# Three value products moved into the preparation of the scan's blocks, fixed places for the scan's matrices, and two gate products in other places

## The chip, the cores and the metric

The kernel runs on one core of a Trainium2 chip, as one program in one launch. The metric is the time of one execution in device microseconds; three executions of the kernel before took 1086.29, 1088.93 and 1091.3 us, the median is 1088.93.

## The reference

One encoder layer is applied to two sequences with the same weights, of 1024 and 256 tokens, 1024 wide, in float32. The kernel treats them as 1280 tokens in 10 blocks of 128 and 20 chunks of 64. After an RMS norm one product with `w_in` gives the inputs of three groups of heads, whose outputs are joined, multiplied with `w_out`, and followed by a small embedding branch and a last norm:

```python
qkv = silu(centred_dwconv(a_qkv, conv_w))          # 5 taps; six heads, 3 x 384 channels
aq, ak, av = split(qkv); aq, ak = l2_normalize(aq), l2_normalize(ak)
o_a = rms_norm(gated_delta_rule(forward) + gated_delta_rule(backward)) * silu(a_gate)
o_b = head_layer_norm(retention(forward) + retention(backward)) * silu(b_gate)
o_c = window_attention(c_q, c_k, c_v, sink) * silu(c_gate)
h = h + concat(o_a, o_b, o_c) @ w_out
h = rms_norm(h + (p @ w_ple) * sigmoid(h @ w_pg))
```

The gated delta rule works chunk by chunk: for each chunk, head and direction a 64 x 64 triangular matrix is inverted, and a scan over the chunks carries a 64 x 64 state. Each scan step needs the inverse, the keys, the values, and three matrices that don't depend on the state: the decayed queries, the masked query-key product, and the decayed keys.

## The kernel before

**Dense products.** Every product with `w_in` is made tile by tile of 128 columns. `load_w` (L134) loads a weight tile by one DMA into the single buffer `raw` and splits it into `hi` and `lo`; `dense` (L171) makes 24 matmuls for each of three stretches of tokens (512, 512, 256): 8 slices of the inner dimension, and for each hi x xh, hi x xl and lo x xh. Then `evac` empties the PSUM bank. One such product is 72 matmuls on TensorE (PE); a stretch of tokens of it is called a block of dense work here.

**Stages.** First the nine tiles of `a_qkv` are made one after the other (L509 to L566, order 3, 4, 5, 0, 1, 2, 6, 7, 8: keys, queries, values). Each has a tail: four taps on VectorE (L525), a sigmoid in three ScalarE passes (L98), a product, and then for keys and queries the normalisation (L530 to L550), for values (L552 to L566) ten transposes, copies into the tile `vt`, and three stores to `VTD`. The tiles work in `ot`, rows 0 to 2 and 3 to 5 in turn.

Then `prep_stream` (L569) prepares the scan, from block 9 down to block 0 and for each of the two directions: gram products into PSUM, their transposes, decay factors `ge` on ScalarE, and from these the tile `at` (what is inverted) and the tile `l2`, which the trace calls `l` (the three matrices of the scan). `at` leaves by five DMAs, `l2` by one (L621), all on SP's queue. Behind blocks 5 and 0 comes `invert` (L399): a chain of some sixty VectorE operations for five blocks and both directions together, in `ot` rows 0 and 1, and a store of the inverse to `YDD`. `ge` shares two buffers with `vt`, and `l2` shares two with a tile of the normalisation.

Beside this run dense products as filler. A table says which, and `spread` (L440) draws from both streams in proportion to their lengths:

```python
PP = ["cq0", "cq1", 6, 7, 3, "ck", "cv", 4, 0, 5]                        # beside prep_stream
PB = [1, 2, "q0"]                                                        # beside attention
RS = [["k0", "v0"], ["q1"], ["k1", "v1"], ["k2"], ["v2"], ["q2"], []]    # beside retention
```

A number is a gate: 0 to 2 of the delta rule, 3 to 5 of retention, 6 and 7 of attention. A gate's `evac` (L464) copies the bank to `sz` (L468), makes the sigmoid in `sg`, multiplies, and for gates 0 to 5 stores `sg` to `GD` (L472); `sz` and `sg` have one buffer each. `cq0`, `cq1`, `ck`, `cv` are attention's, `q`, `k`, `v` are retention's.

Last, two streams are woven: `scan_stream` (L749) joins the halves of the inverses (`join`, L650) and makes 20 steps in both directions (`step`, L693); `fill` (L1089) makes attention with PB, then retention with RS. When both are done, `w_out`, `w_pg` and `w_ple` follow (L1126 on).

**What sets the order.** The engines' instructions are put in order when the program is built, by a scheduler that follows the order of the code, its priorities and a timeline of its own; each engine then works strictly in that order, and so does SP's queue of DMAs. A table entry that moves thus moves rows of every engine.

**The scan's matrices.** In `l2`, of shape (128, 2 chunks, 3 pairs of heads, 3 matrices, 64), the two heads of a pair lie on partitions 0 to 63 (`T`) and 64 to 127 (`B`). A step multiplies a whole 128-partition matrix that holds, for one head, the decayed queries in one half and the query-key product in the other. So matrix 0 holds queries in T and the product in B, matrix 1 the other way round, and each needs its own VectorE call per half (L611, L612, L615).

Of the kernel before, what the change touches and what calls it, by code (L numbers as in the profile page):

```python
# [8 lines left out]
F32 = mybir.dt.float32  # L9
# [8 lines left out]
NB = 10  # L18
NC = 20
# [17 lines left out]
PP = ["cq0", "cq1", 6, 7, 3, "ck", "cv", 4, 0, 5]  # L37
PB = [1, 2, "q0"]
RS = [["k0", "v0"], ["q1"], ["k1", "v1"], ["k2"], ["v2"], ["q2"], []]
# [14 lines left out]
def encoder_kernel(ctx: ExitStack, tc: tile.TileContext, I, O, dbg=None, upto=99):  # L54
# [405 lines left out]
    kreg = {}  # L460

    def product(n):
        if n in GCOL:
# [11 lines left out]
            return [(GCOL[n], 128)], evg  # L475
        if n[0] == "c":
# [19 lines left out]
    with tc.tile_pool(name="pa", reuse_waits="tile", bufs=2) as pa:  # L496
# [12 lines left out]
        order = [3, 4, 5, 0, 1, 2, 6, 7, 8]  # L509
        for i, ti in enumerate(order):  # L510
            z = i % 2
            if i == 2:
                beta_alpha(pa)
# [7 lines left out]

            dense(ahead.pop() if ahead else load_w([(ti * 128, 128)]), evac)
            G.memset(Y[:, 1024:1028], 0.0)
            for j in (0, 1, 3, 4):
                V.scalar_tensor_tensor(out=Y[:, 0:1284], in0=R[:, j:j + 1284], scalar=cw(ti, j),  # L525
                                       in1=Y[:, 0:1284], op0=MUL, op1=ADD)
            sigmoid(Z[:, 0:1284], Y[:, 0:1284])
            tt(V, Z[:, 0:1284], Z[:, 0:1284], Y[:, 0:1284], MUL)
            if ti < 6:
                p, isq = ti % 3, ti < 3  # L530
                S.activation(out=Y[:, 0:1284], in_=Z[:, 0:1284], func=AF.Square)
                for t0, n_t, o in SEGS:
                    for s0 in range(0, n_t, 512):
                        n = min(512, n_t - s0)
                        pn = ps("tr")
                        sq = pa.tile([128, 2, 512], F32R, tag="l2", name=nm("sq"))
                        ys = Y[:, o + s0:o + s0 + n]
                        S.copy(sq[:, 0, :n], ys)
                        tt(V, sq[:, 1, :n], ys, sq[:, 0, :n].bitcast(F32), SUB)
                        mm(pn[:, :n], onesR, sq[:, 0, :n], stop=False)  # L540
                        mm(pn[:, :n], onesR, sq[:, 1, :n], start=False)

                        rr = pa.tile([128, 512], F32, tag="ge", name=nm("rr"))
                        S.activation(out=rr[:, :n], in_=pn[:, :n], func=AF.Ln,
                                     scale=64.0 if isq else 1.0, bias=eps64 if isq else eps)
                        S.activation(out=rr[:, :n], in_=rr[:, :n], func=AF.Exp, scale=-0.5)
                        tt(V, kq[:, p, 1 if isq else 0, t0 + s0:t0 + s0 + n], Z[:, o + s0:o + s0 + n], rr[:, :n], MUL)
                if not isq:
                    nc.sync.dma_start(out=KND[:, :, p, :].rearrange("c p t -> p c t"),
                                      in_=kq[:, p, 0, :].rearrange("p (c t) -> p c t", c=NC))  # L550
            else:
                p = ti - 6  # L552
                for b0 in range(0, NB, 4):
                    nb = min(4, NB - b0)
                    o = b0 * 128 if b0 < 8 else 1028
                    pt = ps("tr")
                    for k in range(nb):
                        nc.tensor.transpose(pt[:, k * 128:(k + 1) * 128], Z[:, o + k * 128:o + (k + 1) * 128], ident)
                    pt4 = pt[:, 0:nb * 128].rearrange("p (b h e) -> p b h e", b=nb, h=2)
                    vt = pa.tile([128, 4, 2, 64], F32, tag="ge", name=nm("vt"))  # L560
                    for r in range(2):
                        rr = slice(64 * r, 64 * r + 64)
                        S.copy(vt[T, 0:nb, r], pt4[rr, :, 1])
                        V.tensor_copy(vt[B, 0:nb, r], pt4[rr, :, 0])
                    nc.sync.dma_start(out=VTD[b0 // 4][:, :, p, :].rearrange("c p e -> p c e"),
                                      in_=vt[:, 0:nb].rearrange("p b r e -> p (b r) e"))  # L566
        if dbg:
            dbg("kq", kq)
        def prep_stream():  # L569
            for b in reversed(range(NB)):  # L570
# [18 lines left out]
                for d in range(2):  # L589
# [661 lines left out]
```

## Time and profile before

| | us |
|---|---|
| Median of 3 executions | 1088.93 |
| The profiled execution | 1093.26 |
| Its span, from first to last instruction | 1091.5 |
| PE busy with matmuls | 1016.7 (93%) |
| VectorE (DVE) busy | 653.5 (60%) |
| ScalarE (ACT) busy | 511.8 (47%) |
| GpSimd (POOL) busy | 239.9 (22%) |
| Mean granted clock of PE | 0.96 of full speed |

The profile is one execution, taken by the hardware profiler. Its page gives busy times per engine, a row of 40 slices, and groups of instructions by line of the code; queries of the trace give the same for a stretch of time, list who waited for whom (an engine's idle time is put down to what ended it), and follow the chain of waits back from the last instruction. Line numbers are those of the kernel; L86 and L89 are helpers that make all matmuls and all two-operand VectorE calls, so there the names of the tiles tell the place (`mm` is the PSUM bank of a dense product, `tr`, `sa`, `sb` those of the smaller ones). SP is the queue from which nearly all DMAs are issued. A busy PE is not PE at its peak: the small matmuls of the scan take longer than their columns need, and the granted clock falls in places.

### The profile page before, as it was taken

How to read it: one execution, taken by the hardware profiler on the slowest of the kernel's cores; microseconds unless marked ns; L12 is line 12 of the kernel's file. 1: busy time of each engine (PE TensorE's matmuls, PEld its weight loads, DVE VectorE, ACT ScalarE, POOL GpSimd, SP SyncE). 2: the span in 40 equal slices, each digit the busy share in tenths (PEclk: the TensorE clock that was granted, in tenths of full speed). 3: DMA queues.
4: the chain of work that ended last, by engine and by line, in shares of the span. 5: the costliest groups of instructions: out<-in, count | busy, mean ns of one | idle time of the engine just before them, and what ended most of it. 6: DMA issues, size and time to landing. Idle time of an engine off the chain costs nothing.

```text
span 1091.5 us, 20976 instructions
## 1 busy us (share of the span) xinstructions
PE 1016.7 (93%) x7859; PEld 811.7 (74%) x7859; DVE 653.5 (60%) x1363; ACT 511.8 (47%) x1194; POOL 239.9 (22%) x406
## 2 busy tenths in 40 slices
PE   4999999999896879989999799999889999999996
PEld 3768878888775757767776677777657888888885
DVE  6766676477899769844756674565884333411333
ACT  7476776577456445334434522323341121444544
POOL 2001000022213011221232525644541000112311
PEclk9999999999999888989999799969889999999998
DMA  7112112367776354453553434563571430300211
GB/s 255 40 44 68 44 39 59 74 172 209 183 184 185 79 134 112 111 107 86 142 151 100 123 88 134 141 165 102 172 237 50 164 107 1 97 1 10 97 77 77
DMA packets 192991, 120.56 MB, mean 110 GB/s; under 512 B 104947, under 2 KB 171803, under 8 KB 192891
## 3 DMA queue, kind: packets, MB, share of 16 engines
q1 hardware_dynamic: 187994, 118.97, 39.9%
q8 instruction: 62, 1.02, 0.4%
q0 software_dynamic: 4896, 0.27, 0.4%
q14 instruction: 39, 0.31, 0.1%
HBM read 76.26 MB, written 42.91 MB: 109 GB/s over the span
## 4 chain that ended last, share of the span: by engine, by line
PE 66%; DVE 13%; DMA 10%; SPq 3%; ACT 3%; issue 3%; POOL 1%; DVEq 0%; ACTq 0%; POOLq 0%
PE mm L86 37%; PE sa L86 15%; PE sb L86 7%; PE tr L86 4%; DVE ot L89 3%; DMA ad<-at 2%; DVE l L89 2%; DMA yd<-ot 1%; DMA gd<-sg 1%; DVE ot L966 1%; SPq L618 1%; DMA yn<-yd 1%; PE tr L848 1%; DMA oo<-od 1%; DMA xt<-in_x_prompt 1%
## 5 line engine op out<-in xcount | busy, mean ns | idle before, releaser
L86 PE MATMUL mm<-xh,whi 128*128 128x512 f32 x720 | 268.1, 372 | 16.4 <-ACT sz L468 13.8
L86 PE MATMUL mm<-xl,whi 128*128 128x512 f32 x720 | 263.8, 366 | 0.0
L86 PE MATMUL mm<-xh,wlo 128*128 128x512 f32 x720 | 263.3, 366 | 0.0
L86 PEld LDWEIGHTS mm<-xh,whi 128*128 128x128 f32 x720 | 138.5, 192 | 42.7 <-ACT sz L468 16.4
L86 PEld LDWEIGHTS mm<-xh,wlo 128*128 128x128 f32 x720 | 138.2, 192 | 21.6 <-issue 0.5
L86 PEld LDWEIGHTS mm<-xl,whi 128*128 128x128 f32 x720 | 138.5, 192 | 20.5 <-issue 0.7
L89 DVE TENSOR_TENSOR ot<-ot 128x1284 f32<-128x1284 f32 (+16 forms) x131 | 87.9, 671 | 20.3 <-ACT ot L102 15.1
L89 DVE TENSOR_TENSOR wlo<-raw,whi 128x1024 fp32r<-128x1024 f32 (+1 forms) x56 | 57.8, 1035 | 26.8 <-ACT whi L1082 14.0
L86 PE MATMUL mm<-whi,xh 128*128 128x512 f32 (+1 forms) x168 | 67.0, 400 | 0.4 <-ACT xh L1038 0.4
L86 PE MATMUL mm<-whi,xl 128*128 128x512 f32 (+1 forms) x168 | 66.3, 395 | 0.3 <-DVE xl L89 0.3
L86 PE MATMUL mm<-wlo,xh 128*128 128x512 f32 (+1 forms) x168 | 66.1, 394 | 0.0
L86 PE MATMUL sa<-wlo,xh 128*128 128x512 f32 (+1 forms) x160 | 62.8, 392 | 0.0
L86 PE MATMUL sa<-whi,xl 128*128 128x512 f32 (+1 forms) x160 | 62.6, 391 | 0.0
L86 PE MATMUL sa<-whi,xh 128*128 128x512 f32 (+1 forms) x160 | 62.4, 390 | 0.0
L89 DVE TENSOR_TENSOR sgm<-sb,sgm 128x512 f32<-128x512 f32 (+1 forms) x21 | 14.0, 666 | 72.6 <-ACT sgm L102 60.3
L525 DVE SCALAR_TENSOR_TENSOR ot<-ot,cols 128x1284 f32<-128x1284 f32 x36 | 55.9, 1552 | 0.6
L86 PE MATMUL sa<-sv,l 128*64 128x64 f32 (+1 forms) x912 | 47.8, 241 | 7.8 <-DVE sv L730 5.2
L86 PEld LDWEIGHTS sa<-sv,l 128*64 128x64 f32 (+1 forms) x912 | 37.4, 147 | 19.9 <-DVE sv L730 6.7
L89 POOL TENSOR_TENSOR sv<-sv,elc 64x192 f32<-64x192 f32 x72 | 41.3, 573 | 39.9 <-PE sa L86 20.5
L89 POOL TENSOR_TENSOR ot<-ot,sgm 128x512 f32<-128x512 f32 x19 | 25.5, 1340 | 99.8 <-DVE sgm L89 98.4
L89 POOL TENSOR_TENSOR vt<-vt,sab 128x192 f32<-128x192 f32 x40 | 21.5, 542 | 96.2 <-DMA vt<-vtd 73.2
L850 ACT COPY pts<-tr 128x384 f32<-128x384 f32 (+1 forms) x40 | 16.8, 439 | 49.5 <-PE tr L848 49.3
(302 smaller groups left out, 2005.7 us busy)
## 6 DMA issues: line engine op xcount, KB each, us to landing
raw<-in_w_in SPq DMA_DIRECT2D x28, 512.0 KB, 3.8
l2d<-l SPq DMA_DIRECT2D x20, 576.0 KB, 3.4
l<-l2d SPq DMA_DIRECT2D x40, 288.0 KB, 3.3
xt<-in_x_prompt SPq DMA_DIRECT2D x8, 512.0 KB, 7.1
ot<-in_x_prompt SPq DMA_DIRECT2D x8, 512.0 KB, 3.5
raw<-in_w_pg SPq DMA_DIRECT2D x16, 256.0 KB, 3.4
yp<-ot SPq DMA_DIRECT2D x8, 512.0 KB, 2.6
ad<-at SPq DMA_DIRECT2D x20, 198.0 KB, 3.9
```

The costliest lines, as they stand in the source:

```text
L86: nc.tensor.matmul(out, lhsT, rhs, start=start, stop=stop)
L89: eng.tensor_tensor(out=out, in0=a, in1=b, op=op)
L525: V.scalar_tensor_tensor(out=Y[:, 0:1284], in0=R[:, j:j + 1284], scalar=cw(ti, j), in1=Y[:, 0:1284], op0=MUL, op1=ADD)
L618: nc.sync.dma_start(out=AGD[d][b // 5][q, 2 * b % 10:2 * b % 10 + 2].rearrange("c p r x -> r (c p) x"), in_=at[32 * q:32 * q + 32, :, :, q ...
L848: nc.tensor.transpose(pt[:, k * 128:(k + 1) * 128], pr[:, k * 128:(k + 1) * 128], ident)
L850: S.copy(pts[h][:, 0:nk * 128], pt[:, 0:nk * 128])
L966: V.scalar_tensor_tensor(out=st[r, b2, h], in0=st[r, b, h], scalar=gs[r, 2 * p + h:2 * p + h + 1], in1=kvt[r, b, h], op0=MUL, op1=ADD)
```

## The change

Three edits are made together.

1. **Values woven in.** The serial loop ends after tile 2. Tiles 6 to 8 become the products "x0", "x1", "x2" and stand first in PP. The loop's body is now a function `conv` that returns an `evac` and a `tail`; for an "x" product, `dense_stream` calls the tail when its third block is through. Group 1's inversion, which writes to `ot` rows 0 and 1, must come after x2's tail, and an assertion says so. The attention's products come later in PP than they did.
2. **Fixed places.** The order within `l2` becomes (128, 2 chunks, 3 matrices, 3 pairs, 64). Matrix 0 is the decayed queries and matrix 1 the query-key product in both halves of the partitions, so one call on 128 partitions writes each. The exchange for the lower half now happens in the store: the upper half leaves by one DMA, the lower by three, one for each matrix. `step` reads the new order.
3. **Gates.** PP loses gate 0, which takes the place of gate 2 in PB; gate 2 goes into RS beside "k2".

```diff
-PP = ["cq0", "cq1", 6, 7, 3, "ck", "cv", 4, 0, 5]
-PB = [1, 2, "q0"]
-RS = [["k0", "v0"], ["q1"], ["k1", "v1"], ["k2"], ["v2"], ["q2"], []]
+PP = ["x0", "x1", "x2", 6, 7, 3, "cq0", "cq1", "ck", "cv", 4, 5]
+PB = [1, 0, "q0"]
+RS = [["k0", "v0"], ["q1"], ["k1", "v1"], ["k2", 2], ["v2"], ["q2"], []]
...
             dense(w, evac, blks=NBLK[i:i + 1])
             yield 10.0 * NBLK[i][1] / 1000
+        if n in vtail:
+            vtail.pop(n)()
+            gone.add(n)
...
+        if n[0] == "x":
+            ti = 6 + int(n[1])
+            evac, vtail[n] = conv(ti, ti % 2)
+            return [(ti * 128, 128)], evac
...
-        order = [3, 4, 5, 0, 1, 2, 6, 7, 8]
+        order = [3, 4, 5, 0, 1, 2]
...
-                        tt(V, l2[T, r, :, 1, :], g3[r][T, :, 64:128], ge[T, 0, r], MUL)
-                        tt(V, l2[B, r, :, 0, :], g3[r][B, :, 64:128], ge[B, 0, r], MUL)
-                    tt(V, l2[:, :, :, 2, :], kc, bc(gl, [128, 2, 3, 64]), MUL)
-                    for h, lr in enumerate((T, B)):
-                        tt(V, l2[lr, :, :, h, :], kq[lr, :, 1, tb].rearrange("p q (c t) -> p c q t", c=2), ge[lr, 1], MUL)
+                        tt(V, l2[:, r, 1], g3[r][:, :, 64:128], ge[:, 0, r], MUL)
+                    tt(V, l2[:, :, 2], kc, bc(gl, [128, 2, 3, 64]), MUL)
+                    tt(V, l2[:, :, 0], kq[:, :, 1, tb].rearrange("p q (c t) -> p c q t", c=2), ge[:, 1], MUL)
...
-                    nc.sync.dma_start(out=L2D[d][b].rearrange("r p q a t -> p r (q a t)"),
-                                      in_=l2.rearrange("p r q a t -> p r (q a t)"))
+                    nc.sync.dma_start(out=L2D[d][b][:, T].rearrange("r p a q t -> p r (a q t)"),
+                                      in_=l2[T].rearrange("p r a q t -> p r (a q t)"))
+                    for a, a2 in ((0, 1), (1, 0), (2, 2)):
+                        nc.sync.dma_start(out=L2D[d][b][:, B, a2].rearrange("r p q t -> p r (q t)"),
+                                          in_=l2[B, :, a].rearrange("p r q t -> p r (q t)"))
...
-                mm(pn[T, p], l2[B, p, 2, :], sv[B, p, 0, :])
+                mm(pn[T, p], l2[B, 2, p, :], sv[B, p, 0, :])
...
-            mm(po3[B, p], l2[:, p, 0, :], sv[:, p, 0, :])
+            mm(po3[B, p], l2[:, 0, p, :], sv[:, p, 0, :])
```

More of the change, by code (lines that the diff above doesn't have):

```diff
@@ L460, in encoder_kernel @@
     kreg = {}
+    gone = set()
+    vtail = {}
     def product(n):
@@ L508, in encoder_kernel, with conv, evac @@
                 G.memset(ot[:, 3 * z, a0:a1], 0.0)
-        order = [3, 4, 5, 0, 1, 2, 6, 7, 8]
[L510 to L513, printed above, removed]
+        order = [3, 4, 5, 0, 1, 2]
+        def conv(ti, z):
             R, Y, Z = ot[:, 3 * z, :], ot[:, 3 * z + 1, :], ot[:, 3 * z + 2, :]
-            def evac(p, t0, n, R=R, Y=Y, ti=ti):
+            def evac(p, t0, n):
                 o = t0 + 2 if t0 < 1024 else t0 + 6
@@ L529, in encoder_kernel @@
[L529 to L566, printed above, removed]
@@ new lines, in tail @@
+            def tail():
+                G.memset(Y[:, 1024:1028], 0.0)
+                for j in (0, 1, 3, 4):
+                    V.scalar_tensor_tensor(out=Y[:, 0:1284], in0=R[:, j:j + 1284], scalar=cw(ti, j),
+                                           in1=Y[:, 0:1284], op0=MUL, op1=ADD)
+                sigmoid(Z[:, 0:1284], Y[:, 0:1284])
+                tt(V, Z[:, 0:1284], Z[:, 0:1284], Y[:, 0:1284], MUL)
+                if ti < 6:
+                    p, isq = ti % 3, ti < 3
+                    S.activation(out=Y[:, 0:1284], in_=Z[:, 0:1284], func=AF.Square)
+                    for t0, n_t, o in SEGS:
+                        for s0 in range(0, n_t, 512):
+                            n = min(512, n_t - s0)
+                            pn = ps("tr")
+                            sq = pa.tile([128, 2, 512], F32R, tag="l2", name=nm("sq"))
+                            ys = Y[:, o + s0:o + s0 + n]
+                            S.copy(sq[:, 0, :n], ys)
+                            tt(V, sq[:, 1, :n], ys, sq[:, 0, :n].bitcast(F32), SUB)
+                            mm(pn[:, :n], onesR, sq[:, 0, :n], stop=False)
+                            mm(pn[:, :n], onesR, sq[:, 1, :n], start=False)
+                            rr = pa.tile([128, 512], F32, tag="ge", name=nm("rr"))
+                            S.activation(out=rr[:, :n], in_=pn[:, :n], func=AF.Ln,
+                                         scale=64.0 if isq else 1.0, bias=eps64 if isq else eps)
+                            S.activation(out=rr[:, :n], in_=rr[:, :n], func=AF.Exp, scale=-0.5)
+                            tt(V, kq[:, p, 1 if isq else 0, t0 + s0:t0 + s0 + n], Z[:, o + s0:o + s0 + n], rr[:, :n], MUL)
+                    if not isq:
+                        nc.sync.dma_start(out=KND[:, :, p, :].rearrange("c p t -> p c t"),
+                                          in_=kq[:, p, 0, :].rearrange("p (c t) -> p c t", c=NC))
+                else:
+                    p = ti - 6
+                    for b0 in range(0, NB, 4):
+                        nb = min(4, NB - b0)
+                        o = b0 * 128 if b0 < 8 else 1028
+                        pt = ps("tr")
+                        for k in range(nb):
+                            nc.tensor.transpose(pt[:, k * 128:(k + 1) * 128], Z[:, o + k * 128:o + (k + 1) * 128], ident)
+                        pt4 = pt[:, 0:nb * 128].rearrange("p (b h e) -> p b h e", b=nb, h=2)
+                        vt = pa.tile([128, 4, 2, 64], F32, tag="ge", name=nm("vt"))
+                        for r in range(2):
+                            rr = slice(64 * r, 64 * r + 64)
+                            S.copy(vt[T, 0:nb, r], pt4[rr, :, 1])
+                            V.tensor_copy(vt[B, 0:nb, r], pt4[rr, :, 0])
+                        nc.sync.dma_start(out=VTD[b0 // 4][:, :, p, :].rearrange("c p e -> p c e"),
+                                          in_=vt[:, 0:nb].rearrange("p b r e -> p (b r) e"))
@@ L567, in encoder_kernel @@
+            return evac, tail
+        for i, ti in enumerate(order):
+            if i == 2:
+                beta_alpha(pa)
+            evac, tail = conv(ti, i % 2)
+            dense(ahead.pop() if ahead else load_w([(ti * 128, 128)]), evac)
+            tail()
         if dbg:
```

11 lines of the change are left out of this document (3 added, 8 removed).

## The prediction

> **What bounds the kernel now.** I read the page first, then a table of stretches, then who TensorE waited for, then VectorE's groups, and last the queue of SP.
>
> ```profile
> span 1091.5 us, 20976 instructions
> PE 1016.7 (93%) x7859; PEld 811.7 (74%) x7859; DVE 653.5 (60%) x1363; ACT 511.8 (47%) x1194; POOL 239.9 (22%) x406
> ```
>
> The page's first lines say that TensorE (PE) is the bound: 1016.7 us of the span are its work, and this change takes no matmul away. What can be won is PE's idle time, 1091.5 - 1016.7 = 74.8 us, and what a lower granted clock costs. So I asked where that idle time lies, by stretches of the program (each engine's busy time, then the granted clock, the DMA engines' busy share and GB/s):
>
> ```profile
> core 0: us, PE busy (x) PEld busy (x) DVE busy (x) ACT busy (x) POOL busy (x), PEclk, DMA share, GB/s
> 180.00:219.00 39.00, 39.00 (x219) 33.17 (x220) 20.24 (x30) 23.18 (x47) 0.00 (x0) 1.00 0.34 78
> 219.00:275.00 56.00, 55.64 (x372) 46.90 (x371) 43.22 (x99) 42.23 (x128) 13.40 (x29) 1.00 0.75 195
> 275.00:329.00 54.00, 49.78 (x322) 41.02 (x322) 48.48 (x106) 29.90 (x103) 10.85 (x24) 1.00 0.73 185
> 329.00:345.00 16.00, 13.51 (x63) 10.44 (x62) 14.54 (x30) 8.74 (x23) 2.41 (x6) 1.00 0.63 192
> 345.00:400.00 55.00, 40.39 (x253) 32.69 (x254) 39.31 (x87) 23.52 (x49) 12.61 (x17) 0.84 0.50 111
> 400.00:440.00 40.00, 36.89 (x393) 30.04 (x392) 35.81 (x67) 22.54 (x45) 4.90 (x4) 0.91 0.42 108
> ...
> 565.00:616.00 51.00, 41.40 (x560) 31.80 (x559) 34.95 (x132) 27.22 (x89) 21.56 (x55) 0.88 0.46 120
> ...
> 705.00:731.00 26.00, 24.51 (x325) 19.12 (x319) 20.20 (x65) 8.20 (x27) 11.75 (x21) 0.67 0.58 158
> ...
> 764.00:805.00 41.00, 33.47 (x339) 24.41 (x335) 32.67 (x79) 15.63 (x45) 23.08 (x28) 0.79 0.62 184
> ```
>
> The first row is the end of the serial products (value tiles 6 to 8): PE never idles there and VectorE (DVE) is half free. The preparation follows (219 to 345): PE loses little, but DVE is busy 48.48 of 54 us in its second half, where the inversion of group 1 joins it. The loss comes just behind: from 345 to 400 PE idles 55 - 40.39 = 14.6 us and its clock falls to 0.84. Two later stretches lose 9.6 us (565 to 616) and 7.5 us (764 to 805); these are scan steps with few dense products or none between them. Who ended PE's waits between 219 and 430 (total, times, longest):
>
> ```profile
> PE mm L86 <- ACT sz L468: 13.8, 6, 5.0
> PE sb L86 <- DVE qlz L89: 5.3, 1, 5.3
> ...
> PE sb L86 <- DVE kst L89: 0.7, 1, 0.7
> ```
>
> `sz` is the copy that empties a gate's PSUM bank; it is late because the gate's single buffers `sz` and `sg` are still held. `qlz` and `kst` are the attention's operands, late because DVE stood in the inversion. What holds `sg`:
>
> ```profile
> ACT sg L100 <- DMA gd<-sg: 34.1, 13, 7.2
> 373.42 9.69 DMA yd<-ot
> ```
>
> The first row is over the whole span: ScalarE (ACT) waits until the gate's store has landed. The second is from the chain of waits: the store of group 1's inverse takes 9.7 us, and a gate's store queues among its bytes.
>
> **The change part by part.** *Values woven.* Three products leave the serial front, two more than before stand in the preparation's list (12 for 10), one gate goes from the preparation's list to the attention's, one from there to retention. The price of a product:
>
> ```profile
> 44.17 0.39 PE L86 MATMUL mm<-xh,whi 128*128 128x512 f32 x1
> 44.40 0.40 PE L86 MATMUL mm<-xl,whi 128*128 128x512 f32 x1
> ```
>
> One matmul of 512 columns follows the other after 0.23 us, so a product (48 of 512 columns, 24 of 256 at half of that) is 48 x 0.233 + 24 x 0.117 = 14.0 us of PE. PE's sum stays what it was: -3 in front, +2 in the preparation, +1 beside retention. Going by the order, the last preparation step now stands behind 48 blocks of dense work (16 products) instead of 51, so everything behind it, the scan first, comes up 14 us of PE work earlier, and that work is spent later as filler.
>
> *Fixed places.* One call per matrix instead of one per half of the partitions. The rows of the present calls (minimum, median, maximum in ns; when they run):
>
> ```profile
> L89 DVE TENSOR_TENSOR l<-sa,ge x73: 339/360/363, 224.8 to 338.6; 64x192 f32<-64x192 f32 x73
> L89 DVE TENSOR_TENSOR l<-kq,ge x38: 543/553/557, 225.7 to 340.0; 64x384 f32<-64x384 f32 x38
> L89 DVE TENSOR_TENSOR at<-sa,ge x36: 356/358/360, 229.0 to 338.0; 128x192 f32<-128x192 f32 x36
> L89 DVE TENSOR_TENSOR l<-kc,ge x19: 552/559/560, 225.2 to 339.0; 128x384 f32<-128x384 f32 x19
> ```
>
> 192 columns cost 0.36 us on 64 and on 128 partitions alike, 384 cost 0.55 and 0.56. Per block and direction the l tile took 4 x 0.36 + 2 x 0.553 + 0.559 = 3.1 us and will take 2 x 0.36 + 0.56 + 0.56 = 1.8; twenty of these save 25 us of DVE. Into the same stage come the value tails:
>
> ```profile
> L525 DVE SCALAR_TENSOR_TENSOR ot<-ot,cols 128x1284 f32<-128x1284 f32 x30 | 46.6, 1552 | 0.5
> L89 DVE TENSOR_TENSOR ot<-ot 128x1284 f32<-128x1284 f32 x8 | 11.9, 1493 | 9.9 <-ACT ot L102 9.9
> L564 DVE COPY vt<-tr 64x256 f32<-64x256 f32 x12 | 5.1, 423 | 13.2 <-ACT vt L563 13.1
> ```
>
> A tail is 4 x 1.55 + 1.49 + 4 x 0.42 and two half copies, about 10 us of DVE; three are 30. So the preparation's DVE work grows by 30 - 25 = 5 us while two more products give it 28 us more room. None of this is on PE's path by itself; its worth is that the inversion of group 1 is no longer late. The order of DVE shows it, where the attention's operands begin (snk, qlz; `ot` rows of 120 partitions are inversion steps, 120x2x17x14 is a part of step 17 of 30):
>
> ```order
> L89 TENSOR_TENSOR l_384_3379<-kq,ge_3366 64x6x64 x2
> L89 TENSOR_TENSOR ot<-ot 120x2x238
> L89 TENSOR_TENSOR ot<-ot 120x2x17x14
> L89 TENSOR_TENSOR ot<-ot 120x2x234
> L89 TENSOR_TENSOR sg_3422<-sg_3422,sz_3423 128x256
> L89 TENSOR_TENSOR ot<-ot 120x2x18x13
> L89 TENSOR_TENSOR ot<-ot 120x2x228
> L794 TENSOR_SCALAR snk<-rvb 128x1 x4
> L800 TENSOR_SCALAR qlz_3753<-ident 64x256
> L89 TENSOR_TENSOR ot<-ot 120x2x19x12
> ```
>
> That was before: the inversion is at steps 17 to 19 of 30, with gates multiplied in between (sg). The same place of the changed kernel:
>
> ```order
> L89 TENSOR_TENSOR ot<-ot 120x2x108
> L89 TENSOR_TENSOR wlo_3211<-raw_3208,whi_3210 128x1024
> L89 TENSOR_TENSOR ot<-ot 120x2x27x4
> L89 TENSOR_TENSOR ot<-ot 120x2x84
> L89 TENSOR_TENSOR ot<-ot 120x2x28x3
> L89 TENSOR_TENSOR ot<-ot 120x2x58
> L812 TENSOR_SCALAR snk<-rvb 128x1 x4
> L818 TENSOR_SCALAR qlz_3648<-ident 64x256
> L89 TENSOR_TENSOR ot<-ot 120x2x29x2
> ```
>
> Now it is at step 28, and the gates 4 and 5 come after it. So I take the waits for qlz and kst as gone (-6.0 us; between 0 and -6.0). Of the six waits for `sz` the longest, 5.0, is the one beside the store of the inverse, which stays; of the other 8.8 us I take off half, since one gate of three goes and no inversion stands before the two that stay: -4.4 (between +5.0, one such wait more where gate 2 now stands, and -8.8). The clock of 0.84 costs 0.16 x 40.39 = 6.5 us of work in 345 to 400; with half of the waits gone I take -3 (0 to -6.5). The Trainium skill, "TensorE: Matmul & The Clock Gate", Part 1, says that the clock halves after an idle window of about 3.4 us and needs as long to return. An estimate from it is 1.7 us for each of two long waits saved, about what I take; that 705 to 731 shows 0.67 with only 1.5 us idle it would not say by itself.
>
> The scan step's matmuls read the same 64 columns of l from other offsets, which changes no count and no length; I cost that at nothing, and there is no cover that could go.
>
> *The scan's filler.* PE's order at the same scan step (the eleventh load of `kn`; kst, pr and pts are the attention's, mm a dense product), before:
>
> ```order
> L86 MATMUL sa_4596<-sv_5975,l_808_6211 64x64 x6
> L86 MATMUL sb_5663<-kst_3723,qh_5656 128x256
> L86 MATMUL sb_5663<-kst_3723,qlz_3753 128x256
> L86 MATMUL sb_5670<-kst_3723,qh_5656 128x256
> L86 MATMUL sb_5670<-kst_3723,qlz_3753 128x256
> L86 MATMUL sa_4596<-sv_6229,kn_6370 64x64 x6
> L86 MATMUL sa_4556<-r_6331,yc_6318 64x64 x6
> L848 MATMUL tr_5497<-ident,pr_5467 128x128 x2
> L848 MATMUL tr_5503<-ident,pr_5474 128x128 x2
> ```
>
> and in the changed kernel:
>
> ```order
> L86 MATMUL sb_5726<-kst_3618,qh_5712 128x256
> L86 MATMUL sb_5726<-kst_3618,qlz_3648 128x256
> L86 MATMUL sa_4451<-sv_6077,l_808_6211 64x64 x5
> L86 MATMUL sa_4491<-sv_6124,kn_6265 64x64 x2
> L866 MATMUL tr_5591<-ident,pr_5561 128x128 x2
> L86 MATMUL sa_4491<-sv_6124,kn_6265 64x64 x4
> L86 MATMUL mm_6918<-xh,whi_6366 128x512
> L86 MATMUL mm_6918<-xl,whi_6366 128x512
> ```
>
> Dense products now stand between steps that had none; but some steps further on, and the last ones, are as bare as they were. Of the 9.6 us idle in 565 to 616 I take a third: -3.2 (0 to -9.6). The stretch at 764 I leave.
>
> *What it adds.* Each l tile is stored by four DMAs instead of one, 60 more on SP's queue, and the value stores (`vtd`) now stand between them. In SP's order, before:
>
> ```order
> L565 DMA vtd_415<-vt_1707 128x8x64
> L565 DMA vtd_416<-vt_1716 128x4x64
> L138 DMA raw_2442<-in_w_in 128x8x128
> L618 DMA agd_1_402<-at_1759 32x6x33 x4
> L620 DMA ad_1_398<-at_1759 128x2x198
> L621 DMA l2d_9_386<-l_187_1760 128x2x576
> L618 DMA agd_1_404<-at_1832 32x6x33 x4
> ```
>
> and after:
>
> ```order
> L631 DMA agd_1_402<-at_1533 32x6x33 x4
> L633 DMA ad_1_398<-at_1533 128x2x198
> L635 DMA l2d_8_385<-l_173_1534 64x2x576
> L638 DMA l2d_8_385<-l_173_1534 64x2x192 x3
> L571 DMA vtd_414<-vt_1593 128x8x64
> L571 DMA vtd_415<-vt_1604 128x8x64
> L138 DMA raw_2281<-in_w_in 128x8x128
> ```
>
> All value stores stood ahead of the first at; now at and l stores and a weight load queue behind a `vtd` that waits for its copy. The rows:
>
> ```profile
> L621 SPq DMA_DIRECT2D l2d<-l x20: 364/413/1604, 222.5 to 341.6; - x20
> 244.70 1.77 SPq L618 DMA_DIRECT2D agd<-at  x4
> l2d<-l SPq DMA_DIRECT2D x20, 576.0 KB, 3.4
> SPq L565 <- DVE vt L564: 37.8, 8, 11.3
> ACT at L607 <- DMA ad<-at: 16.7, 11, 3.3
> ```
>
> An issue takes SP 0.41 us, so 60 more are 25 us of a queue that waited for most of this stage; four stores leave in 1.77 us. The Trainium skill, "DMA: Bandwidth & Descriptors", section "Anatomy of one DMA", gives each DMA a fixed part of about 2.0 us, which speaks against cutting a store into four: taken one behind another, an estimate of 120 us. The row of four in 1.77 us shows that they overlap, so the sum does not use it. The tile `vt` also shares two buffers with `ge`, so nine times a `ge` must wait until a value store has landed. The nearest row, the same kind of wait of `at`, is 16.7 / 11 = 1.5 us; 9 x 1.5 = 14 us on ACT, which is busy 72 of 110 us in 219 to 329. I charge 2 us for all that is added (0 to the rival's price below).
>
> **The sum.** -6.0 - 4.4 - 3.0 - 3.2 + 2.0 = -14.6 us. The profiled execution took 1093.3 us (span 1091.5 and 1.8 around it), so 1078.7; it is 4.3 above the median 1088.9, which makes **1074**. With every term half as large, or half-way to its far bound (all far bounds together: -30.9), this case spans 1066 to 1082.
>
> **The rivals.** *The idle time only moves.* The store of the inverse still holds `sg`, the four gates still come in one run (4, 5, 1, 0 for 4, 0, 5, 1, 2), and PE waits elsewhere for what DVE no longer delays. For it: the 34.1 us of ACT's waits for gate stores. Then only the clock and a part remain, -4: 1085, same.
>
> *DVE becomes the bound of the preparation (slower).* Place: the nine `ge` behind value stores. SP stood 37.8 / 8 = 4.7 us on a `vtd`, a store lands in 3.4; 8.1 us each, 73 us in all. DVE's free time from 219 to 345 is 126 - 106 = 20 us, and grows by 28 - 5 to about 43. From 43 / 9 = 4.8 us each the holds reach PE through late gram and `ge` operands; at 8.1 they cost 30 us: 1104. Against it: PE's order still holds dense blocks around each step, and 1.5 us is what the nearest wait costs.
>
> *All of it goes.* If the whole idle time from 275 to 440 (4.2 + 2.5 + 14.6 + 3.1 = 24.4) and the 6.5 of the clock go: 1088.9 - 30.9 = 1058.
>
> **How the numbers follow.** A measurement of this kernel can tell about 0.5%, 5.4 us, from no change: faster is below 1083.5, slower above 1094.4. Chances: forecast 0.54, all of it goes 0.15, only moved 0.17, DVE bound 0.14. The first two are faster, 0.69; same 0.17; slower 0.14. The range reaches from the large gain (1057) to the end of no change (1094) and leaves out the slower rival and a little below.
>
> **What would show it.** Right: no wait for qlz or kst over 1 us; waits for `sz` below 10 us with the longest still beside `yd<-ot`; the stretch behind the preparation at a clock over 0.9; the l calls 128 partitions wide at 0.36 and 0.56 us; the first scan matmul 15 to 35 us earlier than before. Wrong: PE idle over 10 us inside the preparation with releasers `l`, `ge` or `vt`; ACT waiting for `vtd<-vt` over 30 us; or PE's idle total still above 70 us.

## The result, and the profile after

The changed kernel takes 1105.7 us (median of 4 runs, 1099.9 to 1108.8) where the kernel before took 1090.1 beside it: a ratio of 1.0127, 95% interval 1.0096 to 1.0157. Measured once more with more runs, the ratio was 1.0077 (1.0054 to 1.0100). It is slower by about 1%, not faster by 1.3%. The profiled execution is the fastest of the four (1099.9 us, against 1093.3 in the profile of before), so the two traces show only 6.7 us of the loss. The page's first lines of the changed kernel:

```profile
span 1098.2 us, 20992 instructions
PE 1022.0 (93%) x7859; PEld 812.9 (74%) x7859; DVE 624.4 (57%) x1303; ACT 513.3 (47%) x1194; POOL 240.3 (22%) x406
```

VectorE lost 29 us of work (25 were forecast); TensorE's idle time did not fall: 1098.2 - 1022.0 = 76.2 us for 74.8. By stretches (width, then busy time of PE, PEld, DVE, ACT, POOL, then granted clock, DMA share, GB/s), first of the kernel before:

```profile
219.00:345.00 126.00, 118.93 (x754) 98.36 (x752) 106.25 (x234) 80.87 (x253) 26.65 (x58) 1.00 0.73 191
345.00:446.00 101.00, 83.27 (x724) 67.27 (x726) 80.45 (x164) 47.37 (x97) 18.18 (x24) 0.88 0.46 107
446.00:616.00 170.00, 157.28 (x2124) 123.87 (x2118) 104.14 (x327) 73.16 (x206) 51.73 (x101) 0.94 0.49 119
```

and then of the changed kernel, with three shorter ones that the points below use:

```profile
219.00:345.00 126.00, 109.48 (x653) 90.63 (x652) 87.55 (x192) 69.56 (x209) 29.56 (x56) 0.92 0.71 165
345.00:446.00 101.00, 91.53 (x993) 73.65 (x992) 75.83 (x173) 49.81 (x108) 15.34 (x17) 0.95 0.55 126
446.00:616.00 170.00, 159.21 (x1902) 124.20 (x1898) 94.79 (x289) 69.99 (x192) 44.16 (x91) 0.94 0.43 109
...
345.00:400.00 55.00, 46.86 (x402) 38.42 (x401) 38.15 (x87) 28.03 (x60) 7.61 (x6) 0.91 0.54 121
...
565.00:616.00 51.00, 44.14 (x506) 34.27 (x502) 28.73 (x94) 20.94 (x63) 16.27 (x44) 0.90 0.43 112
275.00:313.00 38.00, 36.08 (x214) 29.84 (x214) 33.48 (x80) 18.60 (x68) 8.27 (x18) 0.91 0.69 158
```

Behind the preparation (345 to 446) PE's idle time fell from 17.7 to 9.5 us and the clock rose from 0.88 to 0.95: the gain that was forecast is there. But in the preparation itself (219 to 345), where PE had lost 7.1 us at full clock, it now loses 16.5, at a clock of 0.92. Who ended PE's waits there and just behind it, in the changed kernel:

```profile
PE mm L86 <- ACT whi L149: 8.5, 1, 8.5
PE mm L86 <- ACT sz L473: 7.4, 2, 7.0
PE sa L86 <- DVE l L89: 4.8, 1, 4.8
PE sb L86 <- ACT ge L616: 2.0, 1, 2.0
```

The longest is new: a dense product that waits for its own weights (`whi`, gate 4's). A second profile of the changed kernel, from the repeated measurement, has the same wait with 8.0 us. The load of these weights, into `raw`, had been issued late. SP's queue around it (start, us, line, transfer, count):

```profile
313.14 3.56 SPq L631 DMA_DIRECT2D agd<-at  x4
316.75 0.44 SPq L633 DMA_DIRECT2D ad<-at  x1
317.29 0.59 SPq L635 DMA_DIRECT2D l2d<-l  x1
317.92 2.16 SPq L638 DMA_DIRECT2D l2d<-l  x3
320.18 2.03 SPq L631 DMA_DIRECT2D agd<-at  x4
322.25 0.44 SPq L633 DMA_DIRECT2D ad<-at  x1
322.79 0.59 SPq L635 DMA_DIRECT2D l2d<-l  x1
323.42 2.14 SPq L638 DMA_DIRECT2D l2d<-l  x3
325.61 0.60 SPq L138 DMA_DIRECT2D raw<-in_w_in  x1
```

Each row begins where the one ahead of it ends: here SP waits for nobody, it issues without a gap. The same queue in the kernel before, some 5 to 10 us earlier:

```profile
307.63 1.96 SPq L618 DMA_DIRECT2D agd<-at  x4
309.64 0.44 SPq L620 DMA_DIRECT2D ad<-at  x1
310.18 0.41 SPq L621 DMA_DIRECT2D l2d<-l  x1
312.68 1.77 SPq L618 DMA_DIRECT2D agd<-at  x4
314.49 0.44 SPq L620 DMA_DIRECT2D ad<-at  x1
315.03 1.60 SPq L621 DMA_DIRECT2D l2d<-l  x1
316.74 0.41 SPq L138 DMA_DIRECT2D raw<-in_w_in  x1
```

Here there are holes (310.6 to 312.7), and weight loads stand three `l` tiles apart (at 277.3, 298.5, 316.7 and 335.8 us). In the changed kernel the load ahead of the late one was issued at 265.9 us: nine tiles and 60 us stand between the two. All rows of 296 to 332 add to 19.1 us of issue time before and to 34.6 of 36 after. A part of the price is in the rows of the stores themselves (minimum, median, maximum in ns):

```profile
L638 SPq DMA_DIRECT2D l2d<-l x60: 574/615/1316, 175.3 to 331.6; - x60
...
L635 SPq DMA_DIRECT2D l2d<-l x20: 586/587/1260, 185.3 to 329.0; - x20
```

A store of a third of the lower half takes SP 0.615 us to issue, where the store of the whole tile took 0.413: 4 for 1 is 0.587 + 3 x 0.615 = 2.4 us a tile for 0.4.

### The profile page after: what moved, and what is told of

Same layout as the page of the kernel before. It is cut to its first block, busy times and chain, and to the rows that moved or that the text cites. A ratio compares the mean times of both kernels' runs of the same rounds, so it can differ in the third digit from the quotient of the medians.

```text
span 1098.2 us, 20992 instructions
## 1 busy us (share of the span) xinstructions
PE 1022.0 (93%) x7859; PEld 812.9 (74%) x7859; DVE 624.4 (57%) x1303; ACT 513.3 (47%) x1194; POOL 240.3 (22%) x406
## 4 chain that ended last, share of the span: by engine, by line
PE 68%; DMA 10%; DVE 9%; SPq 5%; issue 3%; ACT 3%; POOL 1%; DVEq 0%; ACTq 0%; POOLq 0%
PE mm L86 38%; PE sa L86 15%; PE sb L86 7%; PE tr L86 4%; DMA raw<-in_w_in 3%; DMA l2d<-l 2%; DVE ot L89 2%; SPq L638 1%; DVE l L89 1%; PE tr L866 1%; DVE ot L984 1%; DMA yn<-yd 1%; SPq L631 1%; POOL oo L89 1%; PE tr L1191 1%
## 5 line engine op out<-in xcount | busy, mean ns | idle before, releaser
L149 ACT CAST whi<-raw 128x1024 fp32r<-128x1024 f32 x30 | 31.6, 1053 | 28.0 <-DMA raw<-in_w_in 16.1
```

Of the source, the lines that this page charges most:

```text
L149: S.copy(hi, raw)
```

## The experiments

The theories, as the expectations name them. A: SP's issue time bounds the preparation and makes weight loads late. B: the gates' new places cost. C: the woven value tails cost, with their buffers. D: PE's idle time is set elsewhere and only changes its place. E (formed later): the change took dense work away from ahead of the scan's first join. Each run's ratio is to the kernel before, run beside it on the same chip; idle is span less PE's busy time of its one profile. The profiles come from several sets of runs, so spans and idle times compare less well than the ratios.

| run | ratio (95%) | span | PE busy | idle |
|---|---|---|---|---|
| before | 1 | 1091.5 | 1016.7 | 74.8 |
| changed, again | 1.0077 (1.0054 to 1.0100) | 1096.1 | 1016.2 | 79.9 |
| places only | 0.9989 (0.9969 to 1.0009) | 1083.9 | 1012.3 | 71.6 |
| gates only | 1.0056 (1.0037 to 1.0074) | 1095.0 | 1017.1 | 77.9 |
| values only | 1.0109 (1.0091 to 1.0128) | 1102.8 | 1024.7 | 78.1 |
| values, places | 1.0004 (0.9983 to 1.0025) | 1098.3 | 1016.0 | 82.3 |
| values, gates | 1.0061 (1.0039 to 1.0083) | 1097.2 | 1020.4 | 76.8 |
| places, gates | 1.0099 (1.0070 to 1.0129) | 1099.2 | 1016.0 | 83.2 |
| before, four stores | 1.0025 (1.0003 to 1.0047) | 1098.2 | 1024.0 | 74.2 |
| changed, lower stores on GpSimd | 1.0024 (1.0000 to 1.0049) | 1094.9 | 1016.7 | 78.2 |
| changed, weights first | 1.0038 (1.0016 to 1.0060) | 1096.3 | 1016.2 | 80.1 |
| changed, other pace | 1.0061 (1.0040 to 1.0082) | 1094.4 | 1019.6 | 74.8 |
| before, other pace | 0.9995 (0.9975 to 1.0016) | 1096.8 | 1021.8 | 75.0 |
| weights first, old gates | 1.0038 (1.0022 to 1.0054) | 1096.7 | 1019.6 | 77.1 |
| weights first, gate 2 back | 1.0114 (1.0083 to 1.0145) | 1100.4 | 1017.8 | 82.6 |
| weights first, gate 0 back | 1.0052 (1.0033 to 1.0071) | 1098.9 | 1018.9 | 80.0 |
| lower stores on GpSimd, old gates | 1.0036 (1.0019 to 1.0053) | 1098.8 | 1015.5 | 83.3 |
| weights first, lead 20 | 1.0161 (1.0113 to 1.0209) | 1111.0 | 1027.4 | 83.6 |
| before, lead 20 | 1.0141 (1.0108 to 1.0173) | 1109.9 | 1027.9 | 82.0 |

### SP's queue

**Lower stores on GpSimd's queue.**

```diff
                     for a, a2 in ((0, 1), (1, 0), (2, 2)):
-                        nc.sync.dma_start(out=L2D[d][b][:, B, a2].rearrange("r p q t -> p r (q t)"),
+                        nc.gpsimd.dma_start(out=L2D[d][b][:, B, a2].rearrange("r p q t -> p r (q t)"),
```

> The changed kernel, but the three stores of an l tile's lower half are issued by GpSimd and not by SP; all places and products stay as changed. Theory A (SP's issue time bounds the preparation: 60 stores more, about 2.3 us of SP for each of 20 tiles, so a weight load comes late): SP's share is as before, gate 4's weights are there in time, the wait for whi of 8.5 us at 331 goes, and the ratio to the kernel before falls from 1.013 to 0.985 to 1.000. Theory B (the gates' new places cost the lead later): the preparation gets better, but the ratio stays at 1.008 to 1.015. Theory C (the woven value tails cost, whoever issues): 1.008 to 1.015, with the first scan matmul no earlier than 417 us.

Measured 1.0024. Two stretches and PE's longest waits of 219 to 446:

```profile
219.00:345.00 126.00, 116.53 (x710) 96.95 (x710) 83.46 (x184) 74.28 (x221) 53.46 (x99) 0.97 0.76 175
345.00:446.00 101.00, 88.29 (x840) 70.75 (x839) 76.70 (x170) 44.00 (x98) 21.09 (x22) 0.92 0.49 110
```

```profile
PE tr L866 <- DVE pr L863: 6.6, 2, 6.3
PE sa L86 <- DVE l L89: 4.4, 1, 4.4
PE sb L86 <- ACT ge L613: 4.1, 3, 2.9
PE sb L86 <- DVE xn L682: 3.5, 1, 3.5
```

The wait for `whi` is gone, the preparation's idle time falls from 16.5 to 9.5 us and its clock is back at 0.97. Theory A holds for this wait. But the stretch behind gives 3.2 us back: new waits for the attention's `pr` and the first join's `xn`. The ratio is just above A's range, whose upper end is 1.000.

**Weights first.**

```diff
-            nc.sync.dma_start(out=raw[:, :, o:o + w], in_=w_in[:, c0:c0 + w].rearrange("(k p) c -> p k c", p=128))
+            with tc.high_priority():
+                nc.sync.dma_start(out=raw[:, :, o:o + w], in_=w_in[:, c0:c0 + w].rearrange("(k p) c -> p k c", p=128))
```

> The changed kernel, all three parts and four stores on SP, but a weight load is put into SP's queue with priority: by the order no load stands more than 17 rows behind the one ahead of it, where gate 4's stood 37 rows behind. Theory A (what the added stores cost is the late weight load): the wait for whi of 8 us at 331 and its half clock go, 12 us in the preparation, ratio from 1.008 to 0.994 to 1.003. Theory D (the idle time only moves): the wait goes, others come, ratio 1.003 to 1.010.

Measured 1.0038, with all 80 stores still on SP and 31.4 of the 36 us of 296 to 332 spent on issues. Its stretches and waits:

```profile
219.00:345.00 126.00, 115.62 (x711) 96.48 (x709) 82.86 (x187) 71.15 (x213) 22.68 (x50) 0.99 0.73 167
345.00:446.00 101.00, 82.73 (x815) 66.64 (x816) 75.02 (x159) 46.54 (x102) 19.21 (x25) 0.88 0.51 113
```

```profile
PE sb L86 <- DVE xn L683: 16.7, 1, 16.7
PE sa L86 <- DVE l L89: 4.3, 1, 4.3
PE sb L86 <- POOL sv L89: 4.0, 1, 4.0
```

So it is not the issue time as such that PE meets, but the place of one load in a full queue: put ahead, it is in time, and the preparation wins back 6.1 us of idle time and its clock. And behind it 8.8 us are lost, with one wait of 16.7 us for the first join. This is what D said would be seen; the ratio lies in D's range, though its interval reaches into A's, which ends at 1.003. Followed back, the chain of waits that ends at this join runs through SP's queue once more: between 345.8 and 363.4 us most of it is SP's own issues (the stores `yd<-ot` and the loads `an<-ad` take 9.4 us of it), then the load of the inverse (`yn<-yd`) takes until 369.6, and VectorE, which has other work first, makes `xn` at 374.2.

**Four stores in the kernel before.**

```diff
-                    nc.sync.dma_start(out=L2D[d][b].rearrange("r p q a t -> p r (q a t)"),
-                                      in_=l2.rearrange("p r q a t -> p r (q a t)"))
+                    nc.sync.dma_start(out=L2D[d][b][:, T].rearrange("r p q a t -> p r (q a t)"),
+                                      in_=l2[T].rearrange("p r q a t -> p r (q a t)"))
+                    for a in range(3):
+                        nc.sync.dma_start(out=L2D[d][b][:, B, a].rearrange("r p a t -> p r (a t)"),
+                                          in_=l2[B, :, a].rearrange("p r a t -> p r (a t)"))
```

> The kernel before, in which only the one store of an l tile is cut in four of the same bytes, all issued by SP; places of the matrices, products and gates stay as before. Theory A (SP's issues): slower, ratio 1.008 to 1.018, with the last preparation step some 10 to 20 us later and waits of PE for weights in 219 to 345 us. Theories B (gates) and C (values): ratio 0.997 to 1.004, since nothing of theirs is in it.

Measured 1.0025: the cut alone costs 0.25%, a third of the loss or less; that is under A's range and within that of B and C. SP issues 28.3 of 36 us in 296 to 332, and PE waits for no weight load, although one (at 290.6 us) stands eight tiles behind the one ahead of it. The places-only kernel has such a load too (at 310.8 us), for which PE waits 0.3 us. So many stores between two loads are a risk, and not yet a wait: PE waits only where it gets to the load's product before the load is through.

### Parts alone and in pairs

**All three again**, without an edit. 

> The changed kernel once more, word for word, to have its ratio from more runs and beside its parts. If the three parts each bring what they did alone or in pairs (without places 1.006, without the gates' move 1.000, stores off SP 1.002), it stands at 1.003 to 1.008; if the first comparison holds, at 1.010 to 1.016, and then the parts do harm only together.

**Values and gates, no fixed places**: the changed kernel with its second part undone.

```diff
-                        tt(V, l2[:, r, 1], g3[r][:, :, 64:128], ge[:, 0, r], MUL)
+                        tt(V, l2[T, r, :, 1, :], g3[r][T, :, 64:128], ge[T, 0, r], MUL)
+                        tt(V, l2[B, r, :, 0, :], g3[r][B, :, 64:128], ge[B, 0, r], MUL)
...
+                    nc.sync.dma_start(out=L2D[d][b].rearrange("r p q a t -> p r (q a t)"),
+                                      in_=l2.rearrange("p r q a t -> p r (q a t)"))
...
```

> The changed kernel without its second part: values woven and gates moved as changed, but the l tile in its old places with its old six VectorE calls and its one store. Theory A: SP's load is as before, and what the prediction hoped for is left: ratio 0.985 to 1.000. Theories B and C: the cause is still in it, ratio 1.008 to 1.018 (a little worse than the changed kernel by up to 25 us of VectorE that are off the path).

**Values and places, old gates**: the changed kernel with its third part undone.

```diff
-PP = ["x0", "x1", "x2", 6, 7, 3, "cq0", "cq1", "ck", "cv", 4, 5]
-PB = [1, 0, "q0"]
+PP = ["x0", "x1", "x2", 6, 7, 3, "cq0", "cq1", "ck", "cv", 4, 0, 5]
+PB = [1, 2, "q0"]
...
-RS = [["k0", "v0"], ["q1"], ["k1", "v1"], ["k2", 2], ["v2"], ["q2"], []]
+RS = [["k0", "v0"], ["q1"], ["k1", "v1"], ["k2"], ["v2"], ["q2"], []]
```

> The changed kernel with its gates where they stood: gate 0 between 4 and 5 in the preparation's list (13 entries), gates 1 and 2 in the attention's, none beside retention; values woven and four stores stay. Theory A: still slow, ratio 1.008 to 1.018, with a wait of PE for a weight in the preparation. Theory B: the lead of 20 us at 640 us is not given back where gate 2 stood, ratio 0.985 to 1.000. Theory C: as A.

**Values alone**: both of these edits in one kernel. 

> The changed kernel with the woven values alone: gates where they stood, l tile in its old places with one store. Theory B: without the gates' move no loss, 0.992 to 1.001. Theory C (woven value tails and the ge and vt buffers cost): 1.004 to 1.010. Theory D (PE's work and the scan's chain set the time, and an edit ahead of the scan only moves PE's idle time): 0.997 to 1.003, PE's idle total again 72 to 82 us.

**Places alone**: the first of these edits the other way round, in the kernel before. 

> The kernel before with the fixed places alone: one VectorE call per matrix, l tile stored by four DMAs; products and gates as before. Theory A (60 stores more on SP's queue are the price): the cut alone cost 1.0025; the 25 us of VectorE saved are off the path, so 1.000 to 1.004. Theory B (gates' places): 0.997 to 1.002, as nothing of the gates is in it.

**Gates alone**: in the kernel before.

```diff
-PP = ["cq0", "cq1", 6, 7, 3, "ck", "cv", 4, 0, 5]
-PB = [1, 2, "q0"]
+PP = ["cq0", "cq1", 6, 7, 3, "ck", "cv", 4, 5]
+PB = [1, 0, "q0"]
...
-RS = [["k0", "v0"], ["q1"], ["k1", "v1"], ["k2"], ["v2"], ["q2"], []]
+RS = [["k0", "v0"], ["q1"], ["k1", "v1"], ["k2", 2], ["v2"], ["q2"], []]
```

> The kernel before with the gates' move alone: gate 0 goes to the attention's list, gate 2 to retention; values in the serial front, l tile as before. Theory B: this is the cost, 1.004 to 1.012, with the lead at 640 us given back at 707. Theories A, C: 0.998 to 1.002. Theory D: 0.997 to 1.003.

**Places and gates**: the edits of the last two in one kernel. 

> The kernel before with fixed places and the gates' move, without the woven values: the last of the combinations. By the order one weight load stands 49 rows behind the one ahead. Theory A: that load is late, a wait for whi or sz of over 5 us in 290 to 345, ratio 1.004 to 1.012. Theory B (the gates' move costs, 1.006 alone, places -0.001): 1.003 to 1.007.

The table has the results; the changed kernel's second measurement, 1.0077, is at the upper end of the range for parts that bring together what they bring alone. No theory fits all of them. Without the 60 stores it is still slow (values alone 1.0109, with gates 1.0061), so A is not the whole: with the values alone weight loads stand at most three tiles apart, PE never waits for one in the preparation, and the preparation idles 9.3 us. And with the 60 stores it need not be slow: in "values, places" all 80 stores are on SP, no weight load is late, the preparation idles 7.7 us, and the ratio is 1.0004 where A had 1.008 to 1.018. The gates' move costs 0.6% alone, 1.1% with the places and 0.7% with both, but it gains 0.5% with the values alone, so B is not a price either. The values alone cost 1.1% and together with the places nothing that can be told, which fits C, since the places free VectorE; but beside the gates' move the values cost nothing either (1.0061 for 1.0056), and there the places cost up to 0.4%. The parts do not add. In "places, gates" a weight load stands 49 rows of SP's order behind the one ahead, the matching wait (for `wlo`, 3.2 us) is there, though shorter than the 5 us that A had expected, and the kernel is among the slowest: A again, as one wait among others.

**Other pace, of the changed kernel and of the one before.**

```diff
-        for _ in spread((10 * T_PREP + 2 * 32.2, prep_stream()), length(PP)):
+        for _ in spread((10 * T_PREP + 2 * 33.2, prep_stream()), length(PP)):
```

> The changed kernel with one number of the pacing changed (the share reserved for the two inversions, 2 x 33.2 for 2 x 32.2): same work, some 950 rows of TensorE's order moved, gate 4's weight load still 33 rows behind the one ahead. Theory A: 1.004 to 1.012, the wait for whi is still there. Theory D with the order as a lottery: anywhere from 0.997 to 1.012, PE's waits at other places.

> The kernel before with the same number changed: same work, 396 rows of TensorE's order moved. If the order alone moves the time, it differs from 1.000 by 0.004 or more either way; if not, 0.998 to 1.002 and the ratios of the parts can be read as theirs.

1.0061 and 0.9995. A number that changes no work, but 950 and 396 rows of TensorE's order, moves the time within the error of its kernel. By what was expected of the second run, the order alone is not shown to move the time by 0.4%; two trials cannot exclude it. In the changed kernel the wait for `whi` shrank to 3.0 us and one for `sz` grew to 15.8: the time stayed, the wait moved.

### The gates, with the load in time

Weights first in the first three; the gates' lists are edited. **All back**, as in "values and places, old gates" above. **Only gate 2 back:**

```diff
-PB = [1, 0, "q0"]
+PB = [1, 0, 2, "q0"]
...
-RS = [["k0", "v0"], ["q1"], ["k1", "v1"], ["k2", 2], ["v2"], ["q2"], []]
+RS = [["k0", "v0"], ["q1"], ["k1", "v1"], ["k2"], ["v2"], ["q2"], []]
```

**Only gate 0 back:**

```diff
-PP = ["x0", "x1", "x2", 6, 7, 3, "cq0", "cq1", "ck", "cv", 4, 5]
-PB = [1, 0, "q0"]
+PP = ["x0", "x1", "x2", 6, 7, 3, "cq0", "cq1", "ck", "cv", 4, 0, 5]
+PB = [1, "q0"]
```

The fourth has all gates back and, instead of weights first, the lower stores on GpSimd's queue. In the same order:

> Weight loads with priority (as in the run where they are put first) and all gates at their old places; woven values and four stores stay. Theory B (what is left with the load on time, 1.004, is the gates' move): 0.996 to 1.001. Theory D (PE's idle time and half clock only change their place): 1.002 to 1.008, with PE's idle total again 74 us or more.

> Weight loads with priority; gate 0 in the attention's list as changed, but gate 2 there too, behind it, and none beside retention. Theory B with gate 2 as the cause (14 us of dense work stand beside retention, where there is cover already, and lack beside the attention): 0.996 to 1.001, with PE's idle time in 446 to 616 smaller than with gate 2 moved (12.9 us) by 4 us or more. With gate 0 as the cause: 1.003 to 1.007.

> Weight loads with priority; gate 0 back in the preparation's list between 4 and 5, gate 2 beside retention as changed, so that the attention's list has two products only. Theory B with gate 0 as the cause (one product less while the preparation and the inversion of group 1 run): 0.996 to 1.001, idle time of 345 to 446 below 14 us (18.3 with gate 0 moved). With gate 2 as the cause: 1.003 to 1.010.

> The changed kernel with the three lower stores on GpSimd's queue and all gates at their old places. Theories A and B together (stores' issues 0.5%, gates 0.5%, each shown alone): 0.993 to 0.999, the fastest of all. Theory D: 1.000 to 1.005, no better than either alone (1.0024 and 1.0004).

Measured 1.0038, 1.0114, 1.0052, 1.0036. With all gates back nothing is gained over weights first alone (1.0038), and the two cures together are no better than either alone. With gate 0 back, 1.0052, the range for gate 2 as the cause is met, but with gate 2 back the kernel is slower still, beyond the range of either gate. So B falls, and D's numbers are met where it gave some, in the first and the fourth. In all four PE waits 11.7 to 16.8 us once, at 370 to 378, for the first join; in the first of them:

```profile
PE sb L86 <- DVE xn L683: 11.7, 1, 11.7
```

### The cover ahead of the first join

TensorE's order gives a reason for that wait. Between the last preparation step and the first join stand 8.0 blocks of dense work in the kernel before, 5.3 with weights first and 4.0 with the old gates as well: what was taken out of the serial front now stands ahead of the preparation's end, and is missing behind it. The stream of the other work can be given a longer lead over the scan's, with weights first and, as a control, in the kernel before:

```diff
-T_JOIN, T_STEP, T_LEAD, T_KV, T_AV, T_AT, T_SP, T_FIN, JN = 3.0, 10.0, -10.0, 0.8, 4.0, 4.8, 2.0, 2.0, 2
+T_JOIN, T_STEP, T_LEAD, T_KV, T_AV, T_AT, T_SP, T_FIN, JN = 3.0, 10.0, -20.0, 0.8, 4.0, 4.8, 2.0, 2.0, 2
```

> All three parts, weight loads with priority, and the other streams lead the scan's by 20 instead of 10: by TensorE's order 7.7 dense blocks now stand between the last preparation step and the first join (8.0 in the kernel before, 5.3 with the lead of 10, where TensorE waited 16.7 us for the join's operand). Theory E (the change took the cover away that the inverse's store needs, three blocks of 4.7 us): that wait falls below 6 us and with it the half clock behind it, ratio from 1.004 to 0.988 to 0.998. Theory D (the idle time only goes elsewhere): the wait falls, the ratio stays at 1.001 to 1.006.

> The control: the kernel before with the same lead of 20. It has 8.0 dense blocks ahead of the first join either way, only one attention block more, and no long wait for the join. Theory E: 0.998 to 1.002. If the lead helps any kernel, whatever the change did: 0.990 to 0.997.

Measured 1.0161 and 1.0141, both beyond anything expected. The long wait for the join did go, but PE's idle time in 345 to 446 stayed (101 - 81.04 = 20.0 us for 18.3):

```profile
345.00:446.00 101.00, 81.04 (x678) 64.84 (x678) 78.79 (x182) 52.58 (x118) 21.88 (x27) 0.90 0.46 107
```

```profile
PE mm L86 <- ACT sz L474: 11.0, 4, 9.8
PE sb L86 <- ACT qh L843: 8.5, 2, 5.4
```

Gates and attention heads wait in its place. So E named a true difference and not the price. Nor does the count of blocks settle the wait by itself: the changed kernel has 5.0 blocks there, fewer than with weights first, and no wait for the join. The control says that the longer lead costs some 1.4% by itself, in this kernel or the other, so the first run alone could not give E's price; whether a cover given in another way would win the 0.4% back was not tried.

## Why the prediction was wrong

**The gains were right, place by place, and in part by luck.** No wait for `qlz` or `kst` over 1 us is left (-6.0, as taken). `sz` fell from 13.8 to 7.4 us (-6.4 for -4.4), but its longest rose from 5.0 to 7.0. The clock in 345 to 400 is 0.91: 0.09 x 46.86 = 4.2 us for 6.5 (-2.3 for -3.0). In 565 to 616 PE idles 51 - 44.14 = 6.9 us for 9.6 (-2.7 for -3.2). That is -17.4 us where -16.6 were forecast. The mechanism behind the first term is borne out by the parts: with the values alone PE still waits 6.3 us for `qlz`, with values and places no more. The luck is in the stretch behind the preparation: with weights first it idles 18.3 us, hardly other than before (17.7), and with the lower stores on GpSimd 12.7. PE then gets to the first join at 358.2 us (374.9 - 16.7) and finds it not ready, where the changed kernel, held up by the late load, gets there at 370.2 us and finds it ready. So a part of the gain there was had only beside the loss ahead of it. The scan also starts where it was to start, 23 us earlier; its first rows, before and then after:

```profile
439.94 0.33 PE L86 MATMUL sa<-vt,yc 64*64 64x64 f32 x2
```

```profile
416.69 0.91 PE L86 MATMUL sa<-vt,yc 64*64 64x64 f32 x24
```

The calls for `l` are 128 partitions wide at 0.35 and 0.55 us, as costed:

```profile
L89 DVE TENSOR_TENSOR l<-sa,ge x40: 344/349/358, 181.8 to 322.9; 128x192 f32<-128x192 f32 x40
...
L89 DVE TENSOR_TENSOR l<-kc,ge x20: 539/551/558, 174.7 to 323.2; 128x384 f32<-128x384 f32 x20
```

**The step that failed is the charge of 2 us for what the change adds**, and in it the sentence that 60 more issues are "25 us of a queue that waited for most of this stage". Both halves were off. The issues are 0.587 + 3 x 0.615 - 0.413 = 2.0 us more a tile, 40 us in all, since a row for a whole tile does not give the price of a part of it. And the waiting was counted over the stage, when the question was a row: between 296 and 332 SP had 36 - 19.1 = 16.9 us free, and the rows there took 15.5 more, which just fits. But the weight load, one row of the same queue, stood 37 rows behind the one ahead (10 to 13 before; DMAs of one kind in a run count as one row): nine tiles for three. What the additions cost in 219 to 345 by the profile: 16.5 - 7.1 = 9.4 us of idle time, and half clock behind two waits, 0.09 x 36.08 = 3.2 us in 275 to 313 and 2.8 in the rows that follow here: 15 us for the 2 charged. Of these the late load has 8.5 + 2.8 = 11.3. The wait for `l` (4.8 us, with half clock behind it) is not the load's: 4.4 and 4.3 us of it stay in the two runs that cure the load. These two give back 0.4 to 0.5% of the time by their ratios (1.0077 to 1.0038 and 1.0024), some 4 to 6 us, measured in different sets of runs. The rows around the late load (behind the busy times stand the granted clock, the DMA share and GB/s):

```profile
322.00:326.00 4.00, 0.44 (x2) 0.20 (x2) 3.93 (x10) 1.12 (x3) 1.10 (x4) 0.65 0.72 174
326.00:331.00 5.00, 0.00 (x0) 0.00 (x0) 2.56 (x6) 0.80 (x1) 0.55 (x1) 0.50 1.03 216
331.00:336.00 5.00, 4.70 (x11) 3.73 (x12) 4.51 (x15) 4.25 (x9) 1.31 (x5) 0.50 0.92 212
336.00:341.00 5.00, 5.00 (x21) 4.00 (x21) 4.84 (x8) 1.84 (x3) 4.23 (x7) 0.91 0.78 208
```

A wait of 8.5 us is followed by 5 us at half clock: 0.50 x 4.70 + 0.09 x 5.00 = 2.8 us more. The Trainium skill, "TensorE: Matmul & The Clock Gate", Part 1, has the clock halved after an idle window of about 3.4 us and restored after about as long at work; this trace agrees in kind, with about 5 us to the return. The 2.0 us for each DMA that the prediction quoted from the Trainium skill, "DMA: Bandwidth & Descriptors", section "Anatomy of one DMA", stands there for DMAs issued from GpSimd, while these stores were issued from SP; the sum did not use it, and no run here shows it.

**The slower rival was the wrong one.** It put the loss into `ge` behind value stores. SP's waits for `vt` fell from 37.8 to 7.7 us; waits for `l` and `ge` in 219 to 446 are 6.8 us together, under its mark of 10; ACT waits 4.6 us for `vtd<-vt`, under its mark of 30. Of the three marks for "wrong", only the idle total over 70 us (76.2) came up.

**The second failed step is the sum itself.** It added what four places would win as if every wait that goes were time won. The runs with the late load cured show what is left of -14.6 us then: +0.2% to +0.4% (1.0024, 1.0038), no gain. With weights first the idle time of the preparation falls by 6.1 us and that of 345 to 446 rises by 8.8. This is the rival "the idle time only moves", to which 0.17 was given; its price (1085, a gain of 4) was still too hopeful.

**What stays open.** In 20 profiles of the same work PE idles 71.6 to 83.6 us, at other places each time. Only two runs have a ratio under 1, "places only" (0.9989) and the kernel before at another pace (0.9995), and both intervals hold 1: none beat the kernel before for certain. What sets that total was not found: the late load is one wait that was shown; the gates' places and the cover ahead of the first join, as tried here, did not turn out to be another. Why the values alone cost 1.1%, with no added store and no late load, and nothing together with the places, was not found either. Nor do the traces say where all of the 8.5 to 15.6 us of the medians lie. They hold 4.6 to 6.7 us of it, split differently in two executions of the same changed kernel (5.3 us of busy and 1.4 of idle time more in one, 5.1 of idle time in the other).

## What to carry to other kernels

Cost a queue's added issues by the stretch in which a needed load shares it, row by row, not by its waiting over a stage: here the full queue did not cost its issue time but the wait for one load that stood behind the stores. And where a wait goes, look for the next thing that the same engine needs and when it is ready; until that is done, a sum of waits removed is a hope and not a forecast. Before a part is given a price of its own, it is worth timing it alone and in pairs: here the same part won or lost 0.5% to 1% with its company.

## What was not expected of the hardware

A piece of a store is not cheaper to issue on SP's queue than the whole: 0.413 us for a tile of 128 x 2 x 576, 0.587 for its upper half in one, 0.615 for a third of its lower half (0.581 and 0.606 in the kernel before with four stores). And the kernel before itself had medians of 1090.1 and 1090.3 us in two sets of runs, and of 1096.3 to 1097.6 in four others, 0.5 to 0.7% apart, more than several of the effects measured here. Five of these six sets are known to have run on five different chips; whether the chip makes the difference was not tried. The ratios above are each taken within one set.
